# Lag kernel's sum directly behind its products, and VectorE and ScalarE in the program's order through all eight units of a state space layer

## The chip, the cores and the metric

One core of one Trainium2 chip runs the whole program. The metric is the device time of one execution in microseconds (us). TensorE (PE) multiplies matrices, VectorE (DVE) and ScalarE (ACT) work element by element, GpSimd (POOL) does a few small things, and SyncE (SP) issues nearly all DMA. Each engine works through its own list of instructions strictly in order, and an instruction whose input or buffer is not ready holds up all that stand behind it in the same list.

## The reference

Two layers over 512 tokens of 1024 channels: a state space layer with a gated linear unit, a SwiGLU network, a sparse attention layer, and a second SwiGLU network. The change lies in the first of these four, cut here to its core:

```python
def s5_mixer(u, lam_re, lam_im, log_dt, b_re, b_im, c_re, c_im, d_skip, w_glu):
    a_bar = jnp.exp(lam * dt)                              # 64 groups x 64 states, complex
    b_bar = ((a_bar - 1.0) / lam)[..., None] * lax.complex(b_re, b_im)
    bu = jnp.einsum('blgh,gph->blgp', ug, b_bar)           # 16 channels to a group
    _, states = lax.associative_scan(_ssm_combine, (a_seq, bu), axis=1)
    y = jnp.einsum('blgp,ghp->blgh', states, c).real + d_skip * u
    y = jax.nn.gelu(y)
    val, gate = jnp.split(y @ w_glu, 2, axis=-1)
    return val * jax.nn.sigmoid(gate)
```

## The kernel before

The 64 groups of channels go in 8 units of 8 groups (`UN = 8`), and the 512 tokens in 64 chunks of 8. For unit u the parts are these, with the names that rows show:

- `tables(u)`: five VectorE operations make the input table W (L655 to L660), two units ahead. `turned(u)` transposes it in two halves on TensorE (L668), and ScalarE copies each half out (WT, L669). `chunk_inputs` (L679) multiplies it with the tokens U. `tokens` (L609, L617) transposes later tokens into U.
- `lags(u)`: TensorE multiplies W with Cz (L697, eight pairs of matmuls) into a PSUM tile called tr. `lags_out(u)` adds a constant on VectorE (Kd, L703) and issues eight DMA that lay Kd out as the matrix M. `spread` (L687, ScalarE) fills Cz.
- `turns(u)`: six VectorE operations make the rotation E. `turns_out` copies it on ScalarE to ES (L745, L746) and fills RT (L747).
- `scan(u)`: products, sum, two scans, products and four additions on VectorE, which end in the states X (L758 to L773).
- `readout(u)`: six VectorE operations make VV (L790 to L792), of which there is one buffer, so unit u+1's can be written only when unit u's is read.
- `outputs(u)`: TensorE multiplies M with U and X with VV (L800, L801). `gelu` follows on ScalarE (L806). `out(u)` transposes on TensorE (L814) into a tr tile, ScalarE copies the rounded y (L819), and VectorE makes the remainder (L820), which frees that tile.
- `filler`: matmuls of the gated unit (L272 to L274, through `mm3`: W's high part with y, with y's remainder, and W's low part with y), in partial sums over the y's that exist. There are 204 of them up to unit 7, and more behind the units. `refill` fetches their weights with `wblock`: DMA, the high part by ScalarE (w_hi, L263), the low part by VectorE (w_lo, L265).

tr tiles have two PSUM buffers, w_raw two and w_hi and w_lo three each.

What sets the order: a scheduler goes over the program with a model of the time, and moves instructions on each engine. Inside `tc.manual_schedule` the engines named there keep the program's own order. Here these are VectorE and ScalarE, from the head of the layer to the end of unit 0 (L948). TensorE and the DMA queues are the scheduler's throughout, and so are VectorE and ScalarE from unit 1 on.

Of the kernel before, what the change touches and what calls it, by code (L numbers as in the profile page):

```python
# [205 lines left out]
class Trunk:  # L206
# [160 lines left out]
    def s5(self, gain_row, x_ap, lre, lim, ldt, b_re, b_im, c_re, c_im, d_ap, w_glu):  # L367
# [6 lines left out]
        manual = ExitStack()  # L374
# [229 lines left out]
        def tokens(q, dve=()):  # L604

            pu = self.tr()
            for i in range(4):
                g = q % 4 * 8 + 2 * i
                PE.transpose(pu[:, i * P : (i + 1) * P], xn[q // 4][:, g : g + 2].rearrange("p g j h -> p (g j h)"), ident)  # L609
            uv = U[q // 2][:, q % 2 * 8 : q % 2 * 8 + 8].rearrange("p (i g2) c -> p i g2 c", g2=2)  # L610
            pv = pu.rearrange("p (i e c) -> p i e c", i=4, e=2)
            for n, (g2, e) in enumerate(((0, 0), (0, 1), (1, 0), (1, 1))):
                o, i_ = uv[e * NCH : (e + 1) * NCH, :, g2], pv[g2 * NCH : (g2 + 1) * NCH, :, e]
                if n in dve:
                    V.tensor_copy(o, i_)
                else:
                    AC.activation(o, i_, AF.Copy)  # L617
# [24 lines left out]
        def tables(u):  # L642

            gs = slice(u * UGP, (u + 1) * UGP)

            def pw(t):
                return t[:, ::-1, gs].rearrange("p k g -> p g k").unsqueeze(3).to_broadcast(sh4)

            def tb(t):
                return t[:, gs].unsqueeze(2).to_broadcast(sh4)  # L650

            W = self.slot(f"a{8 + u % 2}", [P, 2, UGP, T8, H16], "W")
            k1 = self.scratch(0, sh4, "k1")
            k2 = self.scratch(1, sh4, "k2")
            V.tensor_tensor(k1, tb(Br), pw(qs), op=ALU.mult)  # L655
            V.tensor_tensor(k2, tb(Bs), pw(qi), op=ALU.mult)
            V.tensor_tensor(W[:, 0], k1, k2, op=ALU.subtract)
            k2 = self.scratch(1, sh4, "k2")
            V.tensor_tensor(k2, tb(Bd), pw(qr), op=ALU.mult)
            V.tensor_tensor(W[:, 1], k1, k2, op=ALU.add)  # L660
            return W

        def turned(W):
            WT = self.slot("a12", [P, 2, UGP, P], "WT")
            for i in range(2):
                pt = self.tr()
                for j in range(UGP):
                    PE.transpose(pt[:, j * P : (j + 1) * P], W[:, i, j].rearrange(flat), ident)  # L668
                AC.activation(WT[:, i].rearrange("p a b -> p (a b)"), pt, AF.Copy)  # L669
            return WT  # L670

        def chunk_inputs(u, WT):
            ps = self.lg()
            S4 = ps.rearrange("p (i g c) -> p i g c", i=2, g=UGP)
            for i in range(2):
                for j in range(UGP):
                    for g2 in range(2):
                        hs = slice(g2 * SP, (g2 + 1) * SP)
                        PE.matmul(S4[hs, i, j], lhsT=WT[:, i, j, hs], rhs=Ug((u * UGP + j) * 2 + g2),  # L679
                                  start=True, stop=True)  # L680
            return S4
# [8 lines left out]
        def lags(u, W):  # L690

            cz = CZ[u % 2]
            pk = self.tr()
            for j in range(UGP):
                o = pk[:, j * 2 * H16 : (j + 1) * 2 * H16]
                for i in range(2):
                    PE.matmul(o, lhsT=W[:, i, j].rearrange(flat), rhs=cz[:, i, j].rearrange("p a b -> p (a b)"),  # L697
                              start=i == 0, stop=i == 1)
            return pk

        def lags_out(u, pk):
            Kd = sp.tile([P, NG], F32, name="Kd", bufs=2)
            V.tensor_tensor(Kd, pk[:, :NG], Dd[:, u * NG : (u + 1) * NG], op=ALU.add)  # L703
            M = MM[u % 2]
            for i in range(T8):
                (AC if u == 0 and i % 2 and MACT else nc.sync).dma_start(out=M[0 : (i + 1) * H16, i], in_=Kd[(T8 - 1 - i) * H16 : P])
# [19 lines left out]
        def turns(u):  # L726

            gs = slice(u * UGP, (u + 1) * UGP)
            sh = [P, UGP, 8, 8]
            E = self.tp.tile([P, 2, UGP, NCH], F32, name="E", tag="A")  # L730
            e1 = self.scratch(0, [P, 2, UGP, 8, 8], "e1")
            e2 = self.scratch(1, [P, 2, UGP, 8, 8], "e2")
            for j in range(2):
                g = FG[:, j, 0, gs].unsqueeze(2).to_broadcast(sh)
                V.tensor_tensor(e1[:, j], g, FG[:, 0, 1, gs].unsqueeze(3).to_broadcast(sh), op=ALU.mult)
                V.tensor_tensor(e2[:, j], g, FG[:, 1, 1, gs].unsqueeze(3).to_broadcast(sh), op=ALU.mult)
            w = "p g a b -> p g (a b)"
            V.tensor_tensor(E[:, 0], e1[:, 0].rearrange(w), e2[:, 1].rearrange(w), op=ALU.subtract)
            V.tensor_tensor(E[:, 1], e1[:, 1].rearrange(w), e2[:, 0].rearrange(w), op=ALU.add)
            return E  # L740
# [9 lines left out]
        def scan(u, S4, E, ES, between=None):  # L750
            sh = [P, 2, UGP, NCH]
            X = self.scratch(5 + u % 2, [P, UGP, 2, NCH], "X")
            PL.memset(X[:, :, :, 0:1], 0.0)
            z1 = self.scratch(2, sh, "z1")
            z2 = self.scratch(3, sh, "z2")
            z = self.scratch(4, sh, "z")
            Eb = E[:, 0:1].to_broadcast(sh)
            V.tensor_tensor(z1, S4, Eb, op=ALU.mult)  # L758
            V.tensor_tensor(z2, S4[:, ::-1], ES, op=ALU.mult)
            V.tensor_tensor(z1, z1, z2, op=ALU.add)  # L760
            if between is not None:
                between()
            for i in range(2):
                V.tensor_tensor_scan(z[:, i].rearrange("p g c -> p (g c)"), RT[:, u % 2].rearrange("p g c -> p (g c)"),
                                     z1[:, i].rearrange("p g c -> p (g c)"), 0.0, ALU.mult, ALU.add)
            z1 = self.scratch(2, sh, "z1")
            z2 = self.scratch(3, sh, "z2")
            V.tensor_tensor(z1, z, Eb, op=ALU.mult)
            V.tensor_tensor(z2, z[:, ::-1], ES[:, ::-1], op=ALU.mult)
            for i in range(2):  # L770
                for g2 in range(2):
                    hs = slice(g2 * SP, (g2 + 1) * SP)
                    V.tensor_tensor(X[i * SP : (i + 1) * SP, :, g2, 1:], z1[hs, i, :, : NCH - 1],  # L773
                                    z2[hs, i, :, : NCH - 1], op=ALU.add)
            return X
# [100 lines left out]
        def filler(n):  # L876
            for _ in range(n):
                next(fill, None)
# [14 lines left out]
        W = {0: tables(0)}  # L893
# [4 lines left out]
        pk = lags(0, W[0])  # L898
# [15 lines left out]
        for u in range(UN):  # L914
            more = u + 1 < UN
            X = scan(u, S4[u], E[u], ES[u]) if u else X0
            f = PIECES[u]
            if more:
                E[u + 1] = turns(u + 1)
                WT = turned(W[u + 1])  # L920
            if 0 < u < UN - 2:
                tokens(u + 2)
            if u and more:
                S4[u + 1] = chunk_inputs(u + 1, WT)
            for q in range(2 * u + 3, min(2 * u + 5, UN)):
                normal(q)
            filler(f[0])
            warm_up(u)
            yg = self.slot("a14", [NCH, T8, 8, H16], "yg")
            for b in range(2):  # L930
                gelu(b, outputs(u, b, X, VV), yg)
            if u == 0:
                S4[1] = chunk_inputs(1, WT)
                tokens(2)
            filler(f[1])
            if more:
                pk = lags(u + 1, W[u + 1])
            if u + 2 < UN:
                W[u + 2] = tables(u + 2)
                spread(u + 2)  # L940
            if more:
                VV = readout(u + 1)
                lags_out(u + 1, pk)
            out(u, yg)
            if more:
                ES[u + 1] = turns_out(u + 1, E[u + 1])
            refill(3 if u else 2)
            if u == 0:  # L948
                manual.close()
            filler(GLU_BLOCKS[u] * u - sum(f))  # L950
        xr = []
        xt = x_ap.rearrange("(t p) d -> p t d", p=P)
        for t in range(TB):
# [436 lines left out]
```

## Time and profile before

| what | value |
|---|---|
| three runs | 1293.65, 1295.58, 1293.65 us, median 1293.65 |
| the profiled execution | 1294.01 us, its span 1292.3 us |
| busy over the span | PE 1228.5 us (95%), DVE 769.0 (60%), ACT 543.3 (42%), POOL 152.1 (12%) |

The share of busy time is a mean over stages. The state space layer fills about the first 243 us. In the page's 40 slices of 32.3 us TensorE is busy 5, 5, 8 tenths in the first three, and 9 or more from then on almost throughout, while VectorE is at 8 or 9 tenths in the first five and far below that in the SwiGLU networks.

### The profile page before, as it was taken

The page shows a single profiled execution, that of the slowest core. Times are in us where ns is not written, and L with a number is a line of the kernel's source. Part 1 is how long each engine was busy: PE and PEld are TensorE (multiplying, and loading weights), DVE is VectorE, ACT ScalarE, POOL GpSimd, SP SyncE. Part 2 cuts the span into 40 slices and gives each one's busy share as a digit, 9 for nine tenths or more (in the row PEclk, how much of TensorE's full clock was granted, in tenths as well). Part 3 has the DMA queues.
Part 4 walks back from the last instruction along what each step waited for, and adds up shares of the span by engine and source line. Part 5 has one row for each costly group of instructions (what it writes and reads, how often), then busy time and mean ns, then how long its engine had stood idle before and what let it go on. Part 6 is the DMA issues. An engine that isn't in the chain of part 4 may idle for free.

```text
span 1292.3 us, 18058 instructions
## 1 busy us (share of the span) xinstructions
PE 1228.5 (95%) x6844; PEld 1052.0 (81%) x6844; DVE 769.0 (60%) x1533; ACT 543.3 (42%) x1225; POOL 152.1 (12%) x180
## 2 busy tenths in 40 slices
PE   5589999999999999999999799999999999999998
PEld 4467778888888888889889799988888888888887
DVE  8999958654444443335899977765754444443221
ACT  5655445433322322322573678864532223332221
POOL 2000000000000000004754444510000000000000
PEclk9989999999999999999999899999999999999999
DMA  5021224333333333332213111111433333333341
GB/s 120 10 78 44 72 86 128 98 98 98 98 98 98 98 90 95 101 98 92 82 34 98 50 50 34 42 34 49 120 101 98 98 98 97 95 93 96 110 116 47
DMA packets 189735, 108.02 MB, mean 84 GB/s; under 512 B 7208, under 2 KB 188560, under 8 KB 189584
## 3 DMA queue, kind: packets, MB, share of 16 engines
q1 hardware_dynamic: 189264, 106.70, 28.4%
q8 instruction: 54, 0.88, 0.3%
q14 instruction: 33, 0.27, 0.1%
q10 hardware_dynamic: 384, 0.16, 0.1%
HBM read 102.39 MB, written 2.10 MB: 81 GB/s over the span
## 4 chain that ended last, share of the span: by engine, by line
PE 74%; DVE 9%; ACT 2%; issue 1%; DMA 1%; POOL 0%; ACTq 0%; DVEq 0%; POOLq 0%
PE acc L272 21%; PE acc L273 21%; PE acc L274 21%; PE acc L1051 5%; PE acc L1256 2%; DVE mask L1159 2%; DVE m L1158 2%; PE tr L1245 1%; DVE mask L1146 1%; PE lg L1229 1%; DVE ro L988 1%; DVE pe L1232 1%; PE lg L1228 1%; DVE kl L1106 0%; PE tr L1088 0%
## 5 line engine op out<-in xcount | busy, mean ns | idle before, releaser
L263 ACT ACTIVATE w_hi<-w_raw 128x1024 fp32r<-128x1024 f32 (+5 forms) x208 | 199.9, 963 | 511.7 <-PE acc L273 464.3
L265 DVE TENSOR_TENSOR w_lo<-w_raw,w_hi 128x1024 fp32r<-128x1024 f32 (+6 forms) x179 | 194.1, 1085 | 142.4 <-ACT w_hi L263 141.1
L272 PE MATMUL acc<-h,w_hi 128*128 128x512 f32 x704 | 274.5, 390 | 0.0
L274 PE MATMUL acc<-h,w_lo 128*128 128x512 f32 x704 | 273.9, 389 | 0.0
L273 PE MATMUL acc<-h,w_hi 128*128 128x512 f32 x704 | 273.7, 389 | 0.0
L1051 PE MATMUL acc<-w_hi,h 128*128 128x256 f32 (+1 forms) x896 | 175.5, 293 | 0.8 <-ACT h L284 0.8
L272 PEld LDWEIGHTS acc<-h,w_hi 128*128 128x128 f32 x704 | 132.1, 188 | 27.9 <-issue 0.5
L273 PEld LDWEIGHTS acc<-h,w_hi 128*128 128x128 f32 x704 | 132.1, 188 | 27.7 <-issue 0.5
L274 PEld LDWEIGHTS acc<-h,w_lo 128*128 128x128 f32 x704 | 132.1, 188 | 27.5
L1051 PEld LDWEIGHTS acc<-w_hi,h 128*128 128x128 f32 x896 | 142.3, 194 | 1.4 <-ACT h L284 1.0
L1051 PE MATMUL acc<-w_lo,h 128*128 128x256 f32 (+1 forms) x448 | 127.2, 289 | 0.3 <-POOL w_lo L267 0.3
L339 DVE TENSOR_TENSOR u<-acc,rinv 128x512 f32<-128x512 f32 x44 | 30.4, 691 | 132.4 <-PE acc L274 132.4
L272 PE MATMUL acc<-f,w_hi 128*128 128x512 f32 x272 | 106.4, 391 | 0.0
L274 PE MATMUL acc<-f,w_lo 128*128 128x512 f32 x272 | 105.9, 389 | 0.0
L273 PE MATMUL acc<-f,w_hi 128*128 128x512 f32 x272 | 105.8, 389 | 0.0
L1051 PEld LDWEIGHTS acc<-w_lo,h 128*128 128x128 f32 x448 | 85.8, 193 | 0.9 <-POOL w_lo L267 0.6
L336 DVE TENSOR_TENSOR g<-acc,rinv 128x512 f32<-128x512 f32 x44 | 30.4, 691 | 85.5 <-PE acc L274 85.4
L267 POOL TENSOR_TENSOR w_lo<-w_raw,w_hi 128x1024 fp32r<-128x1024 f32 (+2 forms) x29 | 69.6, 2412 | 48.1 <-ACT w_hi L263 47.2
L274 PEld LDWEIGHTS acc<-f,w_lo 128*128 128x128 f32 x272 | 51.0, 188 | 10.8
L273 PEld LDWEIGHTS acc<-f,w_hi 128*128 128x128 f32 x272 | 51.1, 188 | 10.5
L272 PEld LDWEIGHTS acc<-f,w_hi 128*128 128x128 f32 x272 | 51.1, 188 | 10.3
L272 PE MATMUL acc<-y,w_hi 128*128 128x512 f32 x128 | 51.1, 405 | 2.8 <-ACT y L819 1.9
(296 smaller groups left out, 1987.0 us busy)
## 6 DMA issues: line engine op xcount, KB each, us to landing
w_raw<-in_ffn_w_gate_up_dram SPq DMA_DIRECT2D x88, 512.0 KB, 3.7
w_raw<-in_ffn_w_down_dram SPq DMA_DIRECT2D x32, 448.0 KB, 3.6
w_raw<-in_dsa_w_in_dram SPq DMA_DIRECT2D x26, 512.0 KB, 3.5
w_raw<-in_ffn_w_down_dram SPq DMA_DIRECT2D x16, 512.0 KB, 3.9
w_raw<-in_dsa_w_o_dram SPq DMA_DIRECT2D x16, 256.0 KB, 2.7
w_raw<-in_s_w_glu_dram SPq DMA_DIRECT2D x6, 384.0 KB, 3.4
xc<-in_x_dram SPq DMA_DIRECT2D x8, 256.0 KB, 5.8
xr<-in_x_dram SPq DMA_DIRECT2D x4, 512.0 KB, 3.5
```

Of the source, the lines that this page charges most:

```text
L263: nc.scalar.activation(hi, raw, AF.Copy)
L265: nc.vector.tensor_tensor(lo, raw, hi, op=ALU.subtract)
L267: lo_engine.tensor_tensor(lo, raw, hi, op=ALU.subtract)
L272: mm(out, lhsT=whi, rhs=xx[:, 0], start=start, stop=False)
L273: mm(out, lhsT=whi, rhs=xx[:, 1], start=False, stop=False)
L274: mm(out, lhsT=wlo, rhs=xx[:, 0], start=False, stop=stop)
L336: nc.vector.tensor_tensor(g, ps[0], rinv, op=ALU.mult)
L339: nc.vector.tensor_tensor(u, ps[1], rinv, op=ALU.mult)
L1051: PE.matmul(pt[:, :n], lhsT=h[k][:, l, ts], rhs=ww, start=(k == 0 and i == 0), stop=(k == KT - 1 and i == 2))
L1158: V.max(m8, sc)
L1159: V.match_replace(out=sc, in_to_replace=m8, in_values=sc, imm_value=GONE)
L1256: PE.matmul(po[s, b][:, i * HD : (i + 1) * HD], lhsT=pT[:, j * P : (j + 1) * P], rhs=vv[j][:, (s * 4 + i) * HD : (s * 4 + i + 1) * HD], st ...
```

## The change

Two edits in the loop over the units. `lags_out`, with VectorE's addition Kd and its DMA, stands directly behind `lags`, ahead of `tables` and `readout`, and no longer behind `readout`. And the stretch in which VectorE and ScalarE keep the program's order ends behind the loop, no longer behind unit 0.

```diff
             if more:
-                pk = lags(u + 1, W[u + 1])
+                lags_out(u + 1, lags(u + 1, W[u + 1]))
             if u + 2 < UN:
                 W[u + 2] = tables(u + 2)
                 spread(u + 2)
             if more:
                 VV = readout(u + 1)
-                lags_out(u + 1, pk)
             out(u, yg)
             if more:
                 ES[u + 1] = turns_out(u + 1, E[u + 1])
             refill(3 if u else 2)
-            if u == 0:
-                manual.close()
             filler(GLU_BLOCKS[u] * u - sum(f))
+        manual.close()
```

The first place is VectorE around the end of unit 0 and the scan of unit 1. Before, from the second half of E(1) on:

```order
185 L739 TENSOR_TENSOR E<-e_609,e_610 128x256
186 L655 TENSOR_TENSOR k_695<-hB,qs 128x512
187 L656 TENSOR_TENSOR k_696<-hC,qt 128x512
188 L758 TENSOR_TENSOR z_757<-lg,E 128x512
189 L657 TENSOR_TENSOR W<-k_695,k_696 128x512
190 L659 TENSOR_TENSOR k_700<-hB,qt 128x512
191 L660 TENSOR_TENSOR W<-k_695,k_700 128x512
192 L790 TENSOR_TENSOR VV<-Cst,hC 128x512
193 L791 TENSOR_TENSOR k_708<-Csw,psti 128x512
194 L735 TENSOR_TENSOR e_774<-FG 128x256
195 L736 TENSOR_TENSOR e_775<-FG 128x256
```

And in the changed kernel, from the same instruction on:

```order
184 L739 TENSOR_TENSOR E<-e_609,e_610 128x256
185 L703 TENSOR_TENSOR Kd<-tr,Dd 128x128
186 L655 TENSOR_TENSOR k_705<-hB,qs 128x512
187 L656 TENSOR_TENSOR k_706<-hC,qt 128x512
188 L657 TENSOR_TENSOR W<-k_705,k_706 128x512
189 L659 TENSOR_TENSOR k_710<-hB,qt 128x512
190 L660 TENSOR_TENSOR W<-k_705,k_710 128x512
191 L790 TENSOR_TENSOR VV<-Cst,hC 128x512
192 L791 TENSOR_TENSOR k_718<-Csw,psti 128x512
193 L792 TENSOR_TENSOR VV<-VV,k_718 128x512
```

Kd(1) has moved ahead of W(2), and instructions of the scan and of unit 2's E that stood between those of W and VV are gone from there; each of W and VV now stands next to the one whose result it reads.

The second place is ScalarE around the copy of y of unit 3 (y_1250 before, y_1249 in the changed kernel). Before:

```order
114 L806 ACTIVATE yg<-acc_1169 64x4x8x16
115 L806 ACTIVATE yg<-acc_1179 64x4x8x16
116 L745 ACTIVATE ES<-E 128x256
117 L746 ACTIVATE ES<-E 128x256
118 L819 ACTIVATE y_1250<-tr 128x8x64
119 L669 ACTIVATE WT<-tr 128x512 x2
120 L617 ACTIVATE U_93<-tr 64x4x64 x4
121 L862 ACTIVATE part<-acc_1346 128x512
122 L263 ACTIVATE w_hi<-w_raw 128x640
```

In the changed kernel:

```order
103 L806 ACTIVATE yg<-acc_1178 64x4x8x16
104 L862 ACTIVATE part_982<-acc_1188 128x512
105 L687 ACTIVATE Cz_146<-Cst 64x4x16 x4
106 L819 ACTIVATE y_1249<-tr 128x8x64
107 L745 ACTIVATE ES<-E 128x256
108 L746 ACTIVATE ES<-E 128x256
109 L747 ACTIVATE RT<-r_106 128x4x63
110 L263 ACTIVATE w_hi<-w_raw 128x1024 x2
111 L862 ACTIVATE part_1012<-acc_1268 128x512
112 L669 ACTIVATE WT<-tr 128x512 x2
```

The two blocks of 1024 columns were copied one unit earlier before; now they stand behind the copy of y, and ahead of the copies of WT.

The third place is TensorE directly behind the readout of unit 3. Before:

```order
174 L814 MATMUL tr<-ident,yg 128x64 x8
175 L668 MATMUL tr<-ident,W 128x128 x4
176 L800 MATMUL acc_1385<-M_147,U_92 64x128
177 L272 MATMUL acc_1346<-y_1250,w_hi 128x512
178 L272 MATMUL acc_1360<-y_1250,w_hi 128x512
179 L668 MATMUL tr<-ident,W 128x128 x4
180 L679 MATMUL lg<-U_92,WT 64x64 x8
```

In the changed kernel:

```order
155 L814 MATMUL tr<-ident,yg 128x64 x8
156 L668 MATMUL tr<-ident,W 128x128 x4
157 L272 MATMUL acc_1345<-y_735,w_hi 128x512
158 L273 MATMUL acc_1345<-y_735,w_hi 128x512
159 L272 MATMUL acc_1359<-y_735,w_hi 128x512
160 L273 MATMUL acc_1359<-y_735,w_hi 128x512
161 L800 MATMUL acc_1374<-M_147,U_92 64x128
162 L800 MATMUL acc_1384<-M_147,U_92 64x128
163 L668 MATMUL tr<-ident,W 128x128 x4
```

Where the next two filler matmuls finished sums with the new y, four now open two new sums with the first y (y_735) and with w_hi, the block that ScalarE copies at the second place. The same pattern stands behind the readouts of units 4, 5 and 6.

## Rows read from the trace of the kernel before

**Rows 1.** Busy time by stretch: us, PE, PEld, DVE, ACT, POOL (instructions), granted clock, DMA share, GB/s.

```profile
60.00:76.00 16.00, 9.12 (x76) 7.41 (x77) 15.94 (x31) 11.42 (x30) 0.11 (x1) 0.68 0.25 73
131.00:151.00 20.00, 20.00 (x147) 16.21 (x147) 19.51 (x37) 10.64 (x20) 0.11 (x1) 1.00 0.23 63
188.00:243.00 55.00, 55.00 (x258) 45.34 (x257) 43.20 (x65) 30.77 (x49) 0.00 (x0) 1.00 0.37 109
```

**Rows 2.** All waits of TensorE from 100 to 188 us: total, times, longest.

```profile
PE acc L272 <- ACT y L819: 1.3, 4, 0.6
PE acc L800 <- PE acc L274: 0.8, 1, 0.8
PE acc L273 <- DVE y L820: 0.5, 1, 0.5
```

**Rows 3.** All waits of VectorE from 46 to 176 us.

```profile
DVE VV L790 <- PE acc L801: 2.4, 2, 1.5
DVE y L820 <- ACT y L819: 0.4, 1, 0.4
```

**Rows 4.** VectorE's timeline in unit 0, in the program's order: start, duration, instruction.

```profile
39.52 0.68 DVE L758 TENSOR_TENSOR z<-lg,E 128x512 f32<-128x512 f32 x1
...
46.00 0.69 DVE L790 TENSOR_TENSOR VV<-Cst,hC 128x512 f32<-128x512 f32 x1
46.61 0.68 DVE L791 TENSOR_TENSOR k<-Csw,psti 128x512 f32<-128x512 f32 x1
47.33 0.69 DVE L792 TENSOR_TENSOR VV<-VV,k 128x512 f32<-128x512 f32 x1
```

**Rows 5.** VectorE's timeline in unit 2, in the scheduler's order.

```profile
82.25 0.68 DVE L791 TENSOR_TENSOR k<-Csw,psti 128x512 f32<-128x512 f32 x1
82.86 0.68 DVE L760 TENSOR_TENSOR z<-z,z 128x512 f32<-128x512 f32 x1
...
91.31 1.21 DVE L265 TENSOR_TENSOR w_lo<-w_raw,w_hi 128x1024 fp32r<-128x1024 f32 x1
```

**Rows 6.** VectorE's timeline, the additions that end X of units 1, 3 and 7.

```profile
74.49 1.72 DVE L773 TENSOR_TENSOR X<-z,z 64x252 f32<-64x252 f32 x4
...
109.34 1.72 DVE L773 TENSOR_TENSOR X<-z,z 64x252 f32<-64x252 f32 x4
...
175.16 0.42 DVE L773 TENSOR_TENSOR X<-z,z 64x252 f32<-64x252 f32 x1
```

**Rows 7.** ScalarE's timeline: unit 0 in the program's order, and a wide w_hi later.

```profile
62.70 1.11 ACT L819 ACTIVATE y<-tr 128x512 fp32r<-128x512 f32 x1
63.82 0.42 ACT L745 ACTIVATE ES<-E 128x256 f32<-128x256 f32 x1
...
64.45 0.40 ACT L747 ACTIVATE RT<-r 128x252 f32<-128x252 f32 x1
64.75 1.35 ACT L263 ACTIVATE w_hi<-w_raw 128x512 fp32r<-128x512 f32 x2
...
104.32 1.05 ACT L263 ACTIVATE w_hi<-w_raw 128x1024 fp32r<-128x1024 f32 x1
```

**Rows 8.** TensorE's timeline: lag products, readouts of units 3 and 7, transposes, two filler matmuls.

```profile
56.49 1.97 PE L697 MATMUL tr<-Cz,W 128*128 128x32 f32 x16
...
111.83 0.43 PE L801 MATMUL acc<-VV,X 128*64 128x128 f32 x2
...
118.65 0.66 PE L668 MATMUL tr<-ident,W 128*128 128x128 f32 x4
...
140.66 0.39 PE L272 MATMUL acc<-y,w_hi 128*128 128x512 f32 x1
140.89 0.39 PE L273 MATMUL acc<-y,w_hi 128*128 128x512 f32 x1
...
176.74 0.40 PE L800 MATMUL acc<-M,U 128*64 128x128 f32 x2 [0.82 <-PE acc L274]
...
185.56 0.71 PE L814 MATMUL tr<-ident,yg 64*128 64x64 f32 x8
```

## The prediction

> **What bounds the kernel now.** I read first the busy time by stretch. From 60 to 76 us VectorE is busy 15.94 of 16 us while TensorE is busy 9.12; from 131 to 151 us TensorE has no gap at all and VectorE is busy 19.51 of 20; from 188 to 243 us, with the units done, TensorE runs without a gap until the layer's end [rows 1]. So VectorE sets the pace of the first units, both are full from about 100 us on, and behind unit 7 only TensorE's remaining work counts. The waits say the same: from 100 to 188 us TensorE waits 2.6 us in all, and VectorE 2.8 us from 46 to 176 us [rows 2, 3]. The scheduler has filled VectorE's gaps with instructions of other units.
>
> Hence the measure for the change. TensorE's work is the same before and after, and nothing else ends the layer. Its time changes by what TensorE newly waits, less the waits that vanish. I keep this ledger at the first matmul of two readouts: unit 3's at 111.83 us and unit 7's at 176.74 us [rows 8], each with the filler matmuls that stand ahead of it in TensorE's list. A filler costs 0.23 us (140.66 to 140.89 [rows 8]).
>
> **Edit one, Kd earlier.** It moves one VectorE instruction and eight DMA; nothing is added. M is then there earlier, but no row has TensorE wait for M in units 1 to 6, and the one M wait, 0.8 us ahead of unit 7's readout, is in [rows 2]. Alone it gives at most these 0.8 us. Its price is that tables and readout now queue behind Kd, so behind the lag products.
>
> **Edit two, VectorE.** In the program's order each instruction stands next to the one whose result it reads. Unit 0 already runs so: from L790 to the independent L791 0.61 us pass, from L791 to L792, which reads its result, 0.72 [rows 4]. In the scheduler's order L791 is followed by a foreign L760 after 0.61 [rows 5]. I count about ten such pairs in a unit (one in turns, three or four in tables, two in readout, four in the scan), so 10 x 0.11 = 1.1 us.
>
> [...]
>
> Units 1 to 3 before: X(1) is done at 74.49 + 1.72 = 76.2 us, X(3) at 111.1 [rows 6], so 17.4 us for a unit. In that are three weight blocks, 768 + 1024 + 1024 columns; 1024 take 1.21 us [rows 5], so 1.5 a unit. A unit without them takes 15.9 us, and in the program's order 17.0.
>
> X(1) after: between X(0) at 46.0 and X(1) VectorE did work for later units, which now comes behind X(1): one table product, four table operations at about 0.6 us and six half-size ones for E at about 0.33, together 5.0 us. Against it stand some 1.6 us of dependent pairs and the wait of Kd(1), which VectorE now reaches at about 55.6 us (readout, tables and turns, seventeen instructions, take an estimated 9.6 us from 46.0) while the lag products end at 58.46 less half a us, so 2.4 us [rows 4, 8]. X(1) comes at 76.2 - 5.0 + 1.6 + 2.4 = 75.2 us. X(2) follows after 17.0 + 0.9 for one block, at 93.1. The remainder of y(2) is done a unit less the scan later, 17.0 - 6.5 (39.52 to 46.00 [rows 4]): 103.6 us. It frees the tr buffer for which TensorE's tokens wait. Behind that stand tokens and half a chunk input (1.2 us), 4 fillers, lags (1.97) and 18 fillers, 8.2 us, so the readout of unit 3 starts at 111.8, or 111 if the early units run a little better; I take 111.5. Before it stood at 111.83 with 57 fillers ahead, now 48 are ahead. **Term 1:** -0.3 + 9 x 0.23 = 1.8 us late.
>
> **Edit two, ScalarE and TensorE.** Here the main cost arises. In the program's order the weights of the next fillers are rounded (w_hi) behind y, ES, ES and RT, where the scheduler had done it a unit earlier. TensorE's list has, behind the transposes of y and of half of W, four fillers on exactly that w_hi. Unit 0 shows ScalarE's chain in this order: from y at 62.70 to the start of w_hi at 64.75 us 2.05 us, then 1.05 for 1024 columns [rows 7], 3.1 us, of which the four W transposes cover 0.66 [rows 8]: 2.4 us of idle TensorE. In unit 3 and 5 the copies of part or Cz stand in front of y as well (I take 0.8 and 0.4). With narrower blocks (640, 768, 896 columns, scaled from 1.05) units 3 to 6 cost 3.2 + 2.0 + 2.6 + 2.3 = **10.1 us**, term 2.
>
> Next the other half of the W transposes needs the tr buffer that ScalarE's first WT copy frees, and this stands behind the second w_hi and a part copy: 1.0 + two copies of 512 columns at 0.66 [rows 7] = 2.3 us, less the four fillers and two small matmuls in front (1.3 us), about 0.8 to 1.0 us in units 3, 4 and 5 (unit 6 has narrow cover, I leave it out): **term 3**, 2.5 us, an estimate from these rows.
>
> **Term 4:** before, TensorE waited 2.6 us for y and M [rows 2]. The waits for y vanish, since no filler on the new y stands in front; I take off 2.6.
>
> Sum: 1.8 + 10.1 + 2.5 - 2.6 = 11.8 us; I take **11.4**, since VectorE's early lead may be worth a few tenths more. TensorE then starts the readout of unit 7 at about 193 us with 204 fillers done (before 176.74 with 183): 193 - 176.7 - 21 x 0.23 = 11.5, the same ledger from the other end. Does VectorE add to it? X(4) to X(7) come some 2 us ahead of TensorE's arrival in this walk. VectorE's own stalls (Kd(5), because three of the eight lag pairs stand behind the readout of unit 4, 5 to 6 us; VV(7), behind the readout of unit 6, 3 us) are then waits for TensorE and cost nothing twice.
>
> The profiled execution took 1294.01 us, 0.36 over the median of 1293.65. 1294.01 + 11.4 = 1305.4, so **1305.0 us** against the median.
>
> **Rivals.**
> B, nothing measurable: TensorE does not wait for w_hi, since it comes to those fillers late enough, and only VectorE's dependent pairs count. X(7) is then at 75.2 + 6 x 17.0, plus 8.9 for blocks of 7552 columns, less 3.5 for the tables that unit 6 does not make: 182.6 us, in place of 175.58 [rows 6]. That alone is nearly hidden: before, 21 fillers stood between the readout of unit 7 and its transposes at 185.56 [rows 8], and they would be done in front. Readout, gelu and transposes take 4.9 us, so the transposes start near 187: +1 us, 1294.6. For it speaks that VectorE paces the first units; against it the fixed order of both lists. It decides where the wait for w_hi is under half a us.
> C, faster: the lead of the first units stays. TensorE idles 6.9 of 16 us from 60 to 76 us [rows 1]; the earlier X(1) lets fillers start there, and the 5.0 us of postponed work, less 1.6, is kept down to the end: -3.4, 1290.3 us. It needs Kd(1) without its wait as well as w_hi in time.
> D, slower still: VectorE's stalls are not covered. If TensorE reaches the readouts of units 5 and 7 before X, the 5.5 us of Kd(5) and the 3 us of VV(7) come on top in part: +16, 1310 us, at most 1314. The stretch in which TensorE idles 6.9 us also has a granted clock of 0.68, between the two levels [rows 1]; whether waits of 3 us lower it, no row shows.
>
> **How the numbers follow.** My forecast (1300 to 1309) has 0.60, B and what lies between it and my forecast 0.15, C 0.08, D 0.17. The range 1295 to 1312 leaves out C, the lower half of B and the end of D. Within 0.2% (2.6 us, about what a measurement of this kernel can tell) lies most of B: faster 0.08, same 0.12, slower 0.80.
>
> **What would show it.** In the changed profile the units' part of the layer is longer by about 11 us, and everything from the SwiGLU network on has its old length. TensorE has a wait of 2 to 3 us on w_hi (L263) ahead of L272 in each of units 3 to 6, about 10 us in all, and waits of a us on WT. Right for the early part: X(1) near 75 us and Kd(1) with some 2 us of wait. VectorE's busy time is the same within 1%, while its waits rise from 2.8 to some 15 us, with Kd (L703) and VV (L790) as the largest. The argument falls if TensorE's waits between 100 and 195 us are not above 5 us, or if the readout of unit 7 starts before 185 us.

## The result: 23.6 us slower, about twice the forecast, and the profile after

The changed kernel took 1317.44 us in the median of four runs (1315.9 to 1318.37), the kernel before 1293.8 us beside it: a ratio of 1.0181 with a 95% interval of 1.0166 to 1.0197. The forecast was 1305.0 us with a range of 1295 to 1312, so the sign was right and the size was not. The profiled execution took 1318.05 us with a span of 1316.3, 24.0 us more than the span before.

The page's first part, busy time over the span:

```profile
PE 1244.8 (95%) x6844; PEld 1062.6 (81%) x6844; DVE 772.5 (59%) x1533; ACT 542.8 (41%) x1225; POOL 152.3 (12%) x180
```

TensorE executes the same 6844 matmuls as before, but is busy 16.3 us longer (1228.5 before). The remaining 7.7 us of the 24.0 are idle time. Most of the loss is thus not waiting itself. Where it lies is in the busy time by stretch; the columns are those of [rows 1], and the last column but two is the granted clock. First one row of the kernel before that was not shown, from 46 us to the first matmul of the next stage (L296):

```profile
46.00:243.43 197.43, 181.28 (x1211) 148.15 (x1210) 169.88 (x296) 103.60 (x206) 1.09 (x8) 0.97 0.26 75
243.43:1292.30 1048.87, 1025.70 (x5484) 885.14 (x5482) 558.29 (x1060) 412.39 (x957) 142.24 (x152) 0.99 0.29 85
```

And the changed kernel, the same stretch in pieces and whole:

```profile
60.00:76.00 16.00, 11.46 (x77) 9.39 (x78) 15.61 (x28) 8.96 (x23) 0.11 (x1) 0.61 0.26 76
76.00:94.00 18.00, 15.29 (x114) 12.25 (x113) 17.57 (x33) 9.42 (x22) 0.11 (x1) 0.87 0.16 46
94.00:112.00 18.00, 16.10 (x115) 12.94 (x114) 17.50 (x34) 8.39 (x19) 0.11 (x1) 0.81 0.07 17
112.00:131.00 19.00, 15.08 (x94) 11.68 (x92) 15.68 (x24) 9.67 (x20) 0.11 (x1) 0.82 0.19 51
131.00:151.00 20.00, 17.67 (x115) 14.09 (x114) 11.35 (x22) 8.23 (x17) 0.11 (x1) 0.95 0.07 16
151.00:171.00 20.00, 16.77 (x126) 13.50 (x124) 18.45 (x33) 8.68 (x19) 0.11 (x1) 0.93 0.29 81
171.00:191.00 20.00, 20.00 (x121) 15.88 (x121) 11.61 (x23) 3.06 (x6) 0.00 (x0) 0.78 0.29 82
191.00:212.00 21.00, 18.56 (x93) 14.30 (x93) 12.47 (x22) 6.79 (x13) 0.41 (x2) 0.84 0.26 68
46.00:269.70 223.70, 199.34 (x1210) 160.29 (x1209) 175.55 (x296) 106.88 (x219) 1.08 (x8) 0.89 0.23 66
269.70:1316.30 1046.60, 1023.99 (x5484) 883.61 (x5482) 556.16 (x1060) 412.65 (x957) 142.58 (x152) 1.00 0.29 85
```

The stretch is 26.3 us longer with the same matmuls (the rows count 1211 and 1210): 18.1 us are longer matmuls (199.34 against 181.28), 8.2 us idle; in the later layers, whose code is unchanged, the changed kernel is 2.3 us shorter. (In the runs below that part takes 1046.8 to 1049.5 us, so this is scatter and no gain.) Before, the clock was 1.00 in [rows 1] from 131 us on, and 0.68 only from 60 to 76 us; now it lies between 0.78 and 0.95 from 76 to 212 us. Busy time times one less the clock, summed over the seven rows from 76 to 212 us, is 17.2 us, about the 18.1. Of this, 5.0 us lie from 76 to 112 us, ahead of the first wait that was forecast. The row from 171 to 191 us is the most instructive: TensorE is busy 20.00 of 20 us, which reads like full use, at a clock of 0.78.

TensorE's waits from 100 to 215 us, in answer to [rows 2]:

```profile
PE acc L272 <- ACT w_hi L263: 9.8, 4, 3.2
PE tr L814 <- ACT yg L806: 1.4, 2, 0.7
PE tr L668 <- ACT WT L669: 1.3, 1, 1.3
PE acc L800 <- DMA M<-Kd: 0.7, 1, 0.7
PE acc L272 <- ACT y L819: 0.7, 1, 0.7
PE acc L272 <- DVE VV L792: 0.6, 1, 0.6
```

The wait for w_hi, 9.8 us in four pieces, is the one that was forecast (10.1). What follows it was not. TensorE's timeline behind the readout of unit 3 (start, duration, instruction, wait before it):

```profile
119.08 0.66 PE L668 MATMUL tr<-ident,W 128*128 128x128 f32 x4
122.97 0.79 PE L272 MATMUL acc<-y,w_hi 128*128 128x512 f32 x1 [3.24 <-ACT w_hi L263]
123.57 0.63 PE L273 MATMUL acc<-y,w_hi 128*128 128x512 f32 x1
124.00 0.63 PE L272 MATMUL acc<-y,w_hi 128*128 128x512 f32 x1
...
126.03 1.12 PE L668 MATMUL tr<-ident,W 128*128 128x128 f32 x4
...
129.02 0.39 PE L272 MATMUL acc<-y,w_hi 128*128 128x512 f32 x1
```

ScalarE's timeline beside it, in answer to [rows 7]:

```profile
119.83 1.10 ACT L819 ACTIVATE y<-tr 128x512 fp32r<-128x512 f32 x1
120.95 0.42 ACT L745 ACTIVATE ES<-E 128x256 f32<-128x256 f32 x1
...
121.58 0.40 ACT L747 ACTIVATE RT<-r 128x252 f32<-128x252 f32 x1
121.88 1.99 ACT L263 ACTIVATE w_hi<-w_raw 128x1024 fp32r<-128x1024 f32 x2
```

The mechanism of the forecast is there to the letter: y, ES, ES, RT, then w_hi, while TensorE stands. But the fillers behind the wait follow each other after 0.43 us (124.00 less 123.57) and no longer after 0.23, and four W transposes take 1.12 us in place of 0.66 [rows 8]; at 129 us a filler again takes the 0.39 us of [rows 8] and no longer 0.63. The granted clock in such stretches (us, PE, granted clock, DMA share, GB/s):

```profile
119.70:123.00 3.30, 0.06 (x2) 0.80 0.00 0
123.00:128.00 5.00, 5.00 (x28) 0.50 0.38 111
101.90:108.00 6.10, 6.06 (x46) 0.50 0.00 0
170.00:178.00 8.00, 7.97 (x38) 0.50 0.40 115
```

Read in steps of 0.5 us from 0 to 250 us, the granted clock is 0.50 or 1.00 in 498 of 500 steps before (0.50 in 20) and in 485 of 500 in the changed kernel (0.50 in 96), so the values between, in the longer rows, are mostly mixes of the two: the 0.80 above is 1.00 up to 121.5 us and 0.50 from 122 us on. The clock fell to 0.50 in or behind the waits, and the matmuls that followed, busy without a gap, ran at 0.50 for 5 to 8 us in these rows.

### The profile page after: what moved, and what is told of

Same layout as the page of the kernel before. It is cut to its first block, busy times and chain, and to the rows that moved or that the text cites. A ratio compares the mean times of both kernels' runs of the same rounds, so it can differ in the third digit from the quotient of the medians.

```text
span 1316.3 us, 18058 instructions
## 1 busy us (share of the span) xinstructions
PE 1244.8 (95%) x6844; PEld 1062.6 (81%) x6844; DVE 772.5 (59%) x1533; ACT 542.8 (41%) x1225; POOL 152.3 (12%) x180
## 4 chain that ended last, share of the span: by engine, by line
PE 84%; DVE 10%; ACT 3%; issue 1%; DMA 0%; POOL 0%; SPq 0%; DVEq 0%; ACTq 0%; POOLq 0%
PE acc L272 22%; PE acc L273 21%; PE acc L274 21%; PE acc L1049 10%; PE acc L1254 2%; PE tr L1243 1%; PE acc L800 1%; PE acc L801 1%; PE tr L697 1%; PE lg L679 1%; PE tr L1086 1%; PE lg L1227 1%; DVE pe L1230 1%; PE lg L1226 0%; DVE mask L1157 0%
## 5 line engine op out<-in xcount | busy, mean ns | idle before, releaser
L272 PE MATMUL acc<-y,w_hi 128*128 128x512 f32 x128 | 55.4, 436 | 12.0 <-ACT w_hi L263 9.8
L272 PEld LDWEIGHTS acc<-f,w_hi 128*128 128x128 f32 x272 | 51.1, 188 | 10.3
```

The source lines that it names most:

```text
L272: mm(out, lhsT=whi, rhs=xx[:, 0], start=start, stop=False)
```

## The experiments

Theory 1: TensorE's waits for ScalarE's copies, and the lower granted clock behind each of them, make the loss. Theory 2: VectorE's program order makes it. Theory 3: Kd ahead of tables and readout makes it. All times are medians; the kernel before stood at 1294.0 to 1294.3 us beside them.

**The change taken apart.** e1 and e2 are the two edits alone. e3 and e4 are the changed kernel with one engine in the program's order beyond unit 0, and e12 is e3 with Kd at its old place. The edit of e3 (e4 has `E_.Activation` there):

```diff
+            if u == 0:
+                manual.close()
+                manual.enter_context(tc.manual_schedule(engines={E_.DVE}))
             filler(GLU_BLOCKS[u] * u - sum(f))
```

e1: 

> The first edit alone: Kd directly behind the lag products, and from unit 1 on VectorE and ScalarE in the scheduler's order, as before. Theory 1 (TensorE's waits for ScalarE's w_hi and WT, and the lower granted clock behind each of them, make the 24.0 us of span): TensorE gets no new wait, the time is 1292 to 1296 us, and the clock from 100 us to the end of unit 7 stays at 1.00. Theory 2 (VectorE's program order, with its dependent pairs and its stalls at Kd and VV, sets the length): also 1292 to 1296 us, since the scheduler goes round Kd. Theory 3 (tables and readout that queue behind Kd are the cause): 1305 us or more.

e2: 

> The second edit alone: program order on VectorE and ScalarE through all units, and Kd behind the readout, as before. Theory 1: the waits for w_hi stand as in the changed kernel, and so does the lower clock behind them: 1312 to 1320 us. Theory 2: Kd no longer stands in front of tables and readout, so the 15.3 us in which VectorE waits for lag products fall to under 6, and the time falls to 1300 to 1310 us. Theory 3: under 1300 us.

e3: 

> The changed kernel, but beyond unit 0 only VectorE keeps the program's order, and ScalarE is the scheduler's again. Theory 1: the w_hi that TensorE's next fillers read are copied early, TensorE's waits for ScalarE between 100 us and the end of unit 7 fall under 3 us in all, the granted clock there is above 0.95, and the time is 1294 to 1302 us. Theory 2: VectorE has its dependent pairs and its stalls at Kd and VV as in the changed kernel, so the time is 1312 to 1318 us.

e4: 

> The changed kernel, but beyond unit 0 only ScalarE keeps the program's order, and VectorE is the scheduler's again. Theory 1: TensorE waits 2 to 3 us for w_hi behind the transposes of several units, and after each such wait the granted clock is at 0.50 for some us: 1308 to 1318 us. Theory 2: VectorE's order is that of before, and TensorE's waits of some 2 us a unit are its only cost, without more: 1296 to 1303 us.

e12: 

> VectorE alone in the program's order through all units, ScalarE the scheduler's from unit 1 on, and Kd behind the readout as before. Theory 1: TensorE waits for no w_hi, so 1294 to 1300 us, as with Kd early or better (1302.4). Theory 2: the dependent pairs and the stall at VV remain, 1304 us or more.

Measured; "busy" and "idle" are TensorE's, from 46 us to the first L296, as differences to before (181.3 and 16.2 us):

| kernel | Kd | order kept on | us | ratio, 95% | busy | idle |
|---|---|---|---|---|---|---|
| before | late | neither | 1294.3 | | | |
| e1 | early | neither | 1299.9 | 1.0030 to 1.0064 | +5.2 | +1.9 |
| e3 | early | VectorE | 1302.4 | 1.0048 to 1.0078 | +4.8 | +3.3 |
| e4 | early | ScalarE | 1317.0 | 1.0153 to 1.0191 | +11.3 | +11.7 |
| after | early | both | 1317.4 | 1.0166 to 1.0197 | +18.1 | +8.2 |
| e12 | late | VectorE | 1306.2 | 1.0079 to 1.0109 | +8.9 | +4.2 |
| e2 | late | both | 1306.4 | 1.0081 to 1.0111 | +7.0 | +5.5 |

In the changed kernel ScalarE's order is what costs most: 15.0 us (1317.4 less 1302.4), against 2.5 for VectorE's (1302.4 less 1299.9) and 5.6 for Kd alone. That speaks for theory 1. But e3 came out 0.4 us above its range, with 5.9 us of waits for ScalarE from 100 to 200 us in place of under 3. It has no wait for w_hi, and still the clock is 0.83 from 171 to 191 us, behind a wait of 2.29 us for M. And e4, inside its range, got there only in part by the wait that theory 1 names, 6.1 us for w_hi in two pieces. By the ledger of the prediction e4 is 9.7 us behind at the readout of unit 3 (119.50 us, 48 fillers done), ahead of its first wait for w_hi, and 22.3 us behind at unit 7's. Waits for VectorE come first there, 6.4 us for X and 4.1 us put down to unit 2's E. So w_hi is not the whole of ScalarE's share. The effects don't add up either, and theory 1 missed e1, e2 and e12. In e1, which lies between theories 1 and 3, TensorE waits in the early units, where nothing was expected:

```profile
PE acc L801 <- DVE X L773: 5.0, 1, 5.0
PE tr L668 <- ACT WT L669: 4.7, 1, 4.7
```

In e12 TensorE waits for the tr buffer that Kd frees, since Kd stands behind the readout in VectorE's fixed list:

```profile
PE tr L668 <- DVE Kd L703: 10.1, 5, 4.8
```

So e12 came out where theory 2 had it, by a wait that no theory had named, and there edit one helps: with VectorE in the program's order Kd early gives 1302.4 us in place of 1306.2. In e2, too, theory 2 had the number and theory 1 had not: Kd early costs 11 us when both engines keep the order. In each row of the table the longer matmuls are about 1 to 2.7 times the idle time: in none of them does idle time come without longer matmuls.

**Filling the waits with useless work.** If the lower clock behind the waits is the larger part, a kernel in which TensorE works uselessly during the wait should be faster. e5 repeats the first half of the W transposes, which stands directly ahead of the waiting fillers, four times over; e6 seven times. e7 is e5's addition to the kernel before.

```diff
-                for j in range(UGP):
+                for j in list(range(UGP)) * (4 if i == 0 and more_work else 1):
                     PE.transpose(pt[:, j * P : (j + 1) * P], W[:, i, j].rearrange(flat), ident)
...
-                WT = turned(W[u + 1])
+                WT = turned(W[u + 1], u > 2)
```

e5: 

> The changed kernel with 12 useless transposes added ahead of the fillers that wait for w_hi, in each of units 3 to 6 (the first half of W is transposed four times over): 48 transposes of 0.165 us, 7.9 us more work for TensorE, which falls into 9.8 us of waits for w_hi. Theory 1 (the lower granted clock behind each wait is the larger part of the loss): the waits for w_hi shrink to 2 to 3 us in all, the clock between 100 us and the end of unit 7 rises above 0.90, and the kernel with more work is faster than the changed one, 1305 to 1313 us. Rival (the lower clock does not come from these waits): the work fills the waits and no more, 1317 us, or up to 1325 us where it does not fit.

e6: 

> The same with 24 transposes in each of units 3 to 6, 4.0 us a unit and 15.8 us in all, more than the 9.8 us of waits for w_hi, so that no wait is left there. Theory 1: no lower clock behind them; the work beyond the waits costs 6 us, and the clock gives back more: 1306 to 1315 us. Rival: 1317 + 6 = 1323 us or more.

e7: 

> A control: the kernel before with the same 12 useless transposes in each of units 3 to 6. There TensorE hardly waits in this stretch and its clock is full, so both theories expect the added 7.9 us of work to be paid: 1294 + 8 = 1302 us, from 1299 to 1304.

TensorE's timeline of e5 at the place shown above for the changed kernel:

```profile
115.03 1.97 PE L668 MATMUL tr<-ident,W 128*128 128x128 f32 x16
118.97 0.50 PE L272 MATMUL acc<-y,w_hi 128*128 128x512 f32 x1 [1.98 <-ACT w_hi L263]
119.31 0.39 PE L273 MATMUL acc<-y,w_hi 128*128 128x512 f32 x1
...
120.89 0.66 PE L668 MATMUL tr<-ident,W 128*128 128x128 f32 x4
```

And the clock of its stretches:

```profile
112.00:131.00 19.00, 16.29 (x130) 13.45 (x129) 18.57 (x33) 10.90 (x22) 0.11 (x1) 1.00 0.19 51
46.00:256.00 210.00, 194.03 (x1260) 158.03 (x1258) 175.34 (x296) 106.68 (x220) 1.75 (x8) 0.94 0.24 70
```

e5 took 1307.1 us, 10.3 less than the changed kernel with 48 transposes more in it; e6, with 96 more, took 1310.9, still 6.5 less. In e5 the wait is 1.98 us, the clock stays at 1.00, and the matmuls behind it keep their 0.23 us. From the first W transpose to the waiting filler 3.9 us pass in both kernels (115.03 to 118.97 in e5, 119.08 to 122.97 in the changed kernel), so ScalarE is not faster: the work only fills the wait. The waits for w_hi are 4.5 us in all in e5 and 1.7 in e6, a little more than expected. The rival had 1317 and more, so it falls.

The added transposes come to stand behind the readouts of units 2 to 5; the wait behind unit 6 is not filled, and the clock from 171 to 191 us is 0.83 in both. Not all of the gain comes from w_hi. e5 reaches the readout of unit 3 at 110.44 us, 4.0 us ahead of the changed kernel and before any wait for w_hi. The added transposes behind unit 2 shorten a wait for WT there from 1.29 to 0.89 us, and the clock does not fall. And 1.4 us of the lead stand already at the transposes of y of unit 2 (96.61 against 98.01 us), ahead of the first added one, on the same list; they are luck.

In e7 the same 48 transposes cost nothing that can be measured: 1294.05 us, a ratio of 1.0004 (0.9994 to 1.0013), where 8 us were expected. Sixteen take 1.97 us and four 0.66, so 12 more are 1.3 us and not 2.0, 5.2 us in all; by the first L296 (244.5 against 243.43 us) only 1.1 of them is left. TensorE is busy 2.7 us longer there and idle 1.7 us less, so small gaps took in a part; what became of the rest was not followed up.

**A wait by itself.** e9 puts six waits of rising length into the kernel before, in the first SwiGLU network, where TensorE has no gap (before, it is busy 50.00 of 50 us from 490 to 540 us and again from 540 to 590 us) and a clock of 1.00; in e10 the last line reads the constant `self.ident` in place of `hold`, so nothing waits.

```diff
+            if after is None and 0 < d < KT - 1:
+                p1, p2, hold = self.tr(), self.tr(), self.tmp("A", "hold")
+                for t in range(TB):
+                    nc.tensor.transpose(p1[:, t * P : (t + 1) * P], self.ident, self.ident)
+                nc.vector.tensor_copy(hold, p1)
+                for _ in range(d - 1):
+                    nc.vector.tensor_tensor(hold, hold, hold, op=ALU.mult)
+                nc.tensor.transpose(p2[:, :P], hold[:, :P], self.ident)
```

e9: 

> What a wait of TensorE costs, by itself: the kernel before, with six forced waits in the down projection of the first SwiGLU network, where TensorE has no gap and a granted clock of 1.00. Behind each of the output tiles 1 to 6, TensorE (held there in the program's order) makes four small transposes, VectorE copies them and multiplies the copy 0, 1, 2, 3, 4 or 5 times in a chain of dependent instructions of about 0.7 us, and TensorE transposes the end of the chain. The waits are each longer than the last, from about 1 us to about 6 us, some 20 us in all. Theory 1: behind the longer ones the granted clock falls to 0.50 for some us, and the time rises by clearly more than the waits, 1294 + 20 + 8 to 14 = 1322 to 1328 us. Rival (a wait costs its own length): 1294 + 20 = 1314 us, as much as the waits in its profile sum up to, within 2 us.

e10: 

> The control to the forced waits: the same transposes and the same chains on VectorE, but TensorE's second transpose reads the constant matrix and waits for no chain. Both theories: no wait, full clock, 24 small transposes and six more of about 0.1 us, so 1295 to 1299 us.

TensorE's timeline of e9, the transposes that wait:

```profile
505.23 0.33 PE L373 MATMUL tr<-ident,hold 128*128 128x128 f32 x1 [0.94 <-DVE hold L370]
...
523.65 0.30 PE L373 MATMUL tr<-ident,hold 128*128 128x128 f32 x1 [2.63 <-DVE hold L372]
...
543.28 0.45 PE L373 MATMUL tr<-ident,hold 128*128 128x128 f32 x1 [3.90 <-DVE hold L372]
...
565.15 0.45 PE L373 MATMUL tr<-ident,hold 128*128 128x128 f32 x1 [4.62 <-DVE hold L372]
...
588.67 0.45 PE L373 MATMUL tr<-ident,hold 128*128 128x128 f32 x1 [5.35 <-DVE hold L372]
...
614.66 0.45 PE L373 MATMUL tr<-ident,hold 128*128 128x128 f32 x1 [7.63 <-DVE hold L372]
```

And the stretch from each of the first five to the next tile's end, always the same work (us, PE, granted clock):

```profile
505.23:520.42 15.19, 15.19 (x68) 1.00 0.29 88
523.65:538.78 15.13, 15.13 (x67) 1.00 0.30 86
543.28:559.92 16.64, 16.64 (x67) 0.90 0.24 68
565.15:582.72 17.57, 17.57 (x67) 0.85 0.18 51
588.67:606.43 17.76, 17.76 (x67) 0.84 0.17 48
```

This is a price list of the kind that the prediction lacked, for this place of the kernel. Behind waits of 0.94 and 2.63 us the work takes its 15.1 to 15.2 us; behind 3.90 us 1.5 us more, behind 4.62 and 5.35 us some 2.5 more, at a clock of 0.84 to 0.90. e9 took 1331.8 us and e10 1298.6. By their spans (1330.7 and 1296.5) that is 34.2 us for 25.0 us of waits, so 9.2 us on top (8.2 by the medians), within theory 1's 8 to 14; the waits were 5 us longer than estimated, hence the total above the range. In the three rows from 3.90 us on the clock fell; behind 0.94 and 2.63 us it stayed at 1.00.

**Weights early.** e8 rounds the next weights ahead of gelu and y; e11 is the same with Kd late.

```diff
             filler(f[0])
+            refill(3 if u else 2)
```

e8: 

> The changed kernel, but ScalarE rounds the next weights (w_hi) ahead of gelu and y, and no longer behind y, ES and RT; all else stays in the program's order. Theory 1: no wait of TensorE for w_hi beyond 1 us, the clock from 112 us on above 0.95, and 1296 to 1303 us. Theory 2 (VectorE's program order sets the length, with Kd(5) and VV(7) as its stalls): the stalls stay, so 1308 to 1316 us.

e11: 

> Program order on VectorE and ScalarE through all units, Kd behind the readout as before, and w_hi rounded ahead of gelu and y. Theory 1: the second edit without its waits for w_hi. The run with the second edit alone took 1306.4 us with 5.8 us of such waits and a clock of 0.83 from 171 to 191 us; without both, 1296 to 1300 us. Theory 2 (VectorE's order): as with the second edit alone, 1304 to 1308 us.

e8 took 1307.1 us (1.0077 to 1.0113), between the ranges of both theories, and e11 1309.7 (1.0104 to 1.0134), above both. No wait for w_hi is left among e8's waits from 46 to 215 us; these stand there instead:

```profile
PE acc L272 <- ACT y L819: 5.1, 6, 1.4
PE tr L668 <- ACT WT L669: 4.9, 4, 1.9
PE acc L801 <- DVE X L773: 3.2, 2, 2.3
```

The 10 us between the changed kernel and e8 are the price of the place of w_hi with Kd early. With Kd late the same move costs 3.3 us (1309.7 in e11 against 1306.4 in e2). The 13 us that e8 is still over before are other waits of the same kind, for ScalarE's y and WT above all, with longer matmuls of 9.4 us and 3.7 us more idle time. In e11 it is Kd, 8.2 us, and a late DMA of weights, 3.7 us. Both signs of theory 1 came in e8, no wait for w_hi and a clock of 0.98 from 112 to 200 us, but the time did not: by the ledger e8 is 6.7 us behind at the readout of unit 3 already. A single move in a fixed list did not mend it.

## Why the prediction was wrong in size, by its own steps

**The step that failed** is the measure itself: "TensorE's work is the same before and after, and nothing else ends the layer. Its time changes by what TensorE newly waits, less the waits that vanish." The work is the same in number, and takes 18.1 us longer. The ledger priced every matmul at the full clock (0.23 us for a filler) also behind the waits it had just put in. The clue stood in [rows 1], a clock of 0.68 in the one stretch where TensorE idles much, and rival D noted it and passed over it ("whether waits of 3 us lower it, no row shows"). D's own price came from VectorE's stalls, which cost nothing, so its 1314 at most was too low as well. B and C fall with the 9.8 us of waits for w_hi.

**Term 1**, forecast 1.8 us at the readout of unit 3. It started at 114.48 us with 48 fillers ahead, as many as forecast, so the ledger reads 114.48 - 111.83 + 9 x 0.23 = 4.7. VectorE's part was close: X(1) ended at 72.48 + 1.72 = 74.2 us (forecast 75.2), Kd(1) waited 2.27 us (2.4), X(3) ended at 109.2, after units of 17.9 and 17.1 us (forecast 17.9 and 17.0). A small slip in the working, 1.5 us a unit for the weight blocks where its own figures give 1.7 (2816 columns at 1.21 us for 1024, over two units), changes nothing here. The 2.9 us too many fit the 6.1 us at clock 0.50 from 101.9 us on, half of which are lost, behind a wait of 1.29 us for WT.

**Term 2**, 10.1 us: 9.8, in pieces of 3.24, 2.28, 2.55 and 1.73 us (forecast 3.2, 2.0, 2.6, 2.3). Right in place, cause and size; its consequence was missing.

**Term 3**, 2.5 us for WT in units 3 to 5: not there. The waits for WT came earlier, 3.2 us at 64.5 us and the 1.29 us above.

**Term 4**, 2.6 us of waits that vanish: 0.7 for y and 0.7 for M stayed, and gelu (yg) took 1.4, together 2.8, so nothing came back.

**VectorE's stalls** came where they were described, and larger: Kd(5) waited 8.4 us and VV(7) 3.5 (forecast 5 to 6 and 3), and Kd(7) with 4.6 and VV(4) with 2.8 were not forecast. From 46 to 215 us, in answer to [rows 3]:

```profile
DVE Kd L703 <- PE tr L697: 15.3, 3, 8.4
DVE VV L790 <- PE acc L801: 7.3, 3, 3.5
```

These two lines alone are 22.6 us, where some 15 were forecast for all of VectorE's waits. They cost nothing twice, as forecast: from 100 us on TensorE has no wait for X above.

**The sum at unit 7.** The readout started at 207.34 us with 204 fillers done; the forecast was 193 us and 204. The ledger's 11.5 us became 207.34 - 176.74 - 21 x 0.23 = 25.8. TensorE's part of that which is idle time, 8.2 us, is even below the forecast 11.4.

What stays open: a wait's length alone does not decide whether the clock falls, and neither do the matmuls just ahead of it. Behind 2.63 us in e9, where TensorE had run wide matmuls without a gap, the clock stayed at 1.00; behind 2.55 us at 170 us in the changed kernel, with the small matmuls of readout and transposes ahead, it was 0.50 for 8 us. But e2 has two waits for w_hi behind nearly the same list, a readout, eight or nine fillers and the transposes of y:

```profile
160.23 0.50 PE L272 MATMUL acc<-y,w_hi 128*128 128x512 f32 x1 [2.97 <-ACT w_hi L263]
...
179.97 0.80 PE L272 MATMUL acc<-y,w_hi 128*128 128x512 f32 x1 [2.83 <-ACT w_hi L263]
```

Behind the first and longer one the granted clock was 1.00 (the row from 151 to 171 us), and the filler took 0.50 us. The second lies in the row from 171 to 191 us, at 0.83, and the filler behind it took 0.80 us, as in the changed kernel behind a wait at 0.50 (0.79 at 122.97 us). So a wait of this size may or may not bring the lower clock, and a forecast can only give it a chance. Nor was it tested why Kd early alone (e1) costs 5.6 us; its waits for X and WT are seen, their cause is not. By the ledger that loss is made ahead of the readout of unit 3, where e1 is 8.0 us behind (6.4 at unit 7's).

## What to carry to other kernels

Where TensorE is the bound, a new wait is priced with its length and with the slower matmuls behind it; here the second part was about twice the first (18.1 against 8.2 us). Read the granted clock in every stretch beside the busy time, since 20.00 of 20 us at 0.78 is not full use. And before instructions are pinned to the program's order, look for copies that another engine's next work waits for: here w_hi stood behind y, ES, ES and RT, 2.05 us (119.83 to 121.88). Moving that one copy back (e8) regained 10 of the 23.6 us and no more.

## What the hardware showed that was not expected

More work made the kernel faster: 48 useless transposes ahead of the waits took 10.3 us off the changed kernel. And the same instructions can meet another clock in another run: from 60 to 97 us the changed kernel and e5 have the same list on TensorE, yet the granted clock was 0.61 in one and 0.51 in the other from 60 to 76 us, and 0.87 and 0.96 from 76 to 94 us.
